# Six sums of an MLP block written for GpSimd instead of VectorE, and four pieces of the block in other places

## The chip, the cores and the metric

The kernel runs on one core of one Trainium2 chip. A core has five engines that run their own instruction streams and meet only at semaphores: TensorE (PE, with its weight loads PEld), VectorE (DVE), ScalarE (ACT), GpSimd (POOL) and SyncE (SP). Sixteen DMA engines move data between the core's memory and HBM. The metric is device time in microseconds (us) of one execution.

## The reference

A decoder trunk of two layers over 256 tokens of width 2048, all in fp32. Layer 0 mixes with a gated linear recurrence, layer 1 with attention; after each mixer comes an MLP with a squared ReLU, and then a gated embedding. The part that the change touches is the MLP:

```python
def sq_relu_mlp(u, w_up, w_down):
    hid = jax.nn.relu(u @ w_up)
    return (hid * hid) @ w_down      # w_up 2048 x 8192, w_down 8192 x 2048
```

## The kernel before

**Precision by splitting.** A weight tile arrives from HBM as fp32. ScalarE rounds it into a tile `whi` (line 113, a CAST), VectorE subtracts to get the remainder `wlo` (line 114), and TensorE makes three products of the parts. The helper `split` records both lines, and there are four buffers of each of `whi` and `wlo`: the cast of a tile waits until TensorE is done with the tile four places ahead of it. A product therefore waits for DMA, ScalarE and VectorE in that order, and the three engines work only a few tiles ahead of TensorE.

**The MLP in blocks.** The hidden width is cut into eight blocks of 1024. For a block, `up` is called eight times: 48 matmuls for 128 hidden columns, then on VectorE the ReLU and the norm's scale (line 304), on ScalarE the square (306), and the split of the squares into `hid` (237, 238). The down projection of a block is not done as eight plain products but in the manner of Strassen and Winograd: a product of two by two parts is made from seven products of half the size, for which sums of parts are formed first.

- Sums of the activations: after every second `up`, lines 317, 318 and 319 form four combinations of `squares` into `scr` (128x256, then twice 128x128), lines 321 (ScalarE) and 322 (VectorE) split them.
- Sums of the weights: many are made by the transfer itself (`accum_op=ALU.add` in `load`, line 283, issued from GpSimd's queue into `chain` and `chq`). Three are made by an engine: line 403 adds the two halves of `chain` (two instructions of 128x1024), line 429 adds a freshly loaded `raw` to `chq`, and line 436 adds a part of `chain` to it (128x1536 each).

The pieces of a block's down projection have names: `p1` to `p7` (two weight tiles of 1024 columns each, 12 matmuls of 512 columns), `r1` to `r7` (tiles of 1024 and 512 columns, 9 matmuls), `m0` and `m1` (one tile, 12 matmuls). Most leave their product in a bank `pp`, from which VectorE adds it into an accumulator (line 338); `r2`, `r3`, `r4`, `m0` and `m1` accumulate in banks `pn` that stay.

**The order.** While block b's `up` products run, block b-1's pieces run between them, in the order of one list of words (line 467). TensorE follows it exactly, since every matmul there is tied behind the one before. For the other engines a scheduler orders the instructions when the kernel is built, by modelled times; at run time each engine takes its own in that order, and an instruction that waits holds up all that stand behind it on the same engine. Two of the sums, 429 and 436, are also tied behind the last `wlo` (`behind`, line 104).

Of the kernel before, what the change touches and what calls it, by code (L numbers as in the profile page):

```python
# [14 lines left out]
ALU = mybir.AluOpType  # L15
# [20 lines left out]
def yoco_kernel(ctx, tc, a, out):  # L36
    nc = tc.nc
# [43 lines left out]
    def slot_flat(which, name, back=0):  # L81

        pool, shift = (late, 28) if which == "C" else (big, 60)
        t = pool.tile([P, KC * 2 * T + 64], F32R, name=name, tag="slot" + which, bufs=1)
        return t[:, shift - back : shift - back + KC * 2 * T]


    def load_slab(src, n, parts, before=None):

        raw = wp.tile([P, D], F32, name="raw", tag="raw", bufs=3)  # L90
        m = n // parts
        if not before:
            nc.sync.dma_start(raw[:, :n], src)
        got = []
        for i in range(parts):
            r = raw[:, i * m : (i + 1) * m]
            if before:
                before[i]()
                nc.sync.dma_start(r, src[:, i * m : (i + 1) * m])
            got.append(split(r, m))  # L100
        return got
# [3 lines left out]
    def behind(ins, name):  # L105

        tc.add_manual_dep(ins.ins, order[name].name, mybir.DependencyInfo(mybir.DependencyClass.NoSync, mybir.DependencyReason.DATA), reason="order")
# [28 lines left out]
    def mm_split(pairs, act, kcs=KC, off=0, ps=None, mm=nc.tensor.matmul):  # L136
        if ps is None:
            ps = psm.tile([P, T], F32, name="ps", tag="mm")
        for k in range(kcs):
            kk = k + off  # L140
            pair, kl = pairs[kk // 8], kk % 8
            st, sp = k == 0, k == kcs - 1
            mm(ps, wk(pair, kl, 0), act[:, k, 0, :], start=st, stop=False)  # L143
            mm(ps, wk(pair, kl, 0), act[:, k, 1, :], start=False, stop=False)  # L144
            mm(ps, wk(pair, kl, 1), act[:, k, 0, :], start=False, stop=sp)  # L145
        return ps
# [103 lines left out]
    def mlp(layer, u, stats, slots, u2, g2, pool, pps):  # L250
# [21 lines left out]
        chq = pool.tile([P, 1536], F32, name="chq", tag="chq", bufs=1)  # L272
        cq = cB[:, :1536]
# [17 lines left out]
        def up(b, i):  # L291

            n = i // 2 + i % 2 * 4
            if n == 0:
                f = slot_flat(slots[b % 2], f"hid{layer}_{b}", 0 if b == NBL - 1 else 24)
                nf = f[:, : 8 * 2 * T].rearrange("p (k w t) -> p k w t", w=2, t=T)
                sf = f[:, 8 * 2 * T :].rearrange("p (j f w t) -> p j f w t", j=4, f=4, w=2)
                hid[b] = nf, sf
            nf, sf = hid[b]
            ps = mm_split(load_slab(a["w_up"][layer, b * 8 + n], D, 2), u, mm=line)  # L300
            if not rs:
                rs.append(stats.rstd())
            t = scr[:, :T]
            nc.vector.scalar_tensor_tensor(t, ps, 0.0, rs[0], op0=ALU.max, op1=ALU.mult)
            s = squares[:, i % 2, :]
            nc.scalar.activation(s, t, AF.Square)
            plain_split(nf, n, s)
            if b == NBL - 1:
                return
            if n < 4:  # L310
                return

            x = scr[:, T:].rearrange("p (f t) -> p f t", f=4)
            a11, a12 = (squares[:, i, :P] for i in range(2))
            a21 = squares[:, 0, P:].unsqueeze(1).broadcast_to([P, 2, P])
            both = squares.rearrange("p i t -> p (i t)").rearrange("p (g t) -> p g t", t=P)[:, 0::3]
            nc.vector.tensor_tensor(x[:, 0:2], a21, both, op=ALU.subtract)
            nc.vector.tensor_tensor(x[:, 2], a11, x[:, 1], op=ALU.subtract)
            nc.vector.tensor_tensor(x[:, 3], a12, x[:, 2], op=ALU.subtract)
            o = sf[:, n - 4]  # L320
            nc.scalar.copy(o[:, :, 0, :], x)
            nc.vector.tensor_tensor(o[:, :, 1, :], x, o[:, :, 0, :].bitcast(F32), op=ALU.subtract)
# [31 lines left out]
        def halves(r):  # L354
            return chunks(r, 4)
# [11 lines left out]
        def down(b):  # L367

            nf, sf = hid[b]

            def plain(half, tok):
                return lambda j: tuple(nf[:, 4 * half + j, w, tok * P : (tok + 1) * P] for w in range(2))

            def form(i):
                return lambda j: tuple(sf[:, j, i, w, :] for w in range(2))

            def one(name, op, pairs):
                o = psm.tile([P, 512], F32, name="pp", tag="mm")
                product(o, op, pairs, True)
                into(name, o)  # L380

            last = b == NBL - 2
            add = dict(accum_op=ALU.add)

            def p1():
                load(nc.gpsimd, cA, quarter(b, 0, 0))
                load(nc.gpsimd, cB, quarter(b, 1, 4))
                pairs = halves(cA)
                load(nc.gpsimd, cA, quarter(b, 0, 4), **add)
                one("1", plain(0, 0), pairs)  # L390

            def p3():
                one("3", form(S4), halves(cB))

            def p2():
                one("2", plain(1, 0), loaded(quarter(b, 1, 0)))

            def p5():
                one("5", form(S1), halves(cA))

                for i in range(2):
                    v, w = (x.rearrange("p (n k c) -> p k n c", n=4, k=4)[:, 2 * i : 2 * i + 2] for x in (cA, cB))
                    nc.vector.tensor_tensor(v, v, w, op=ALU.add)
                load(nc.gpsimd, cB, quarter(b, 0, 4), **add)

            def p7():
                one("7", form(S3), halves(cB))
                load(nc.gpsimd, cq, quarter(b, 1, 12, f=fr))

            def p6():  # L410
                pairs = halves(cA)
                load(nc.gpsimd, cA, quarter(b, 1, 0), **add)
                one("6", form(S2), pairs)

            def p4():
                one("4", plain(1, 1), halves(cA))

            def r1():
                load(nc.gpsimd, chq, quarter(b, 0, 8, f=fr))
                pairs = chunks(chq, 3)  # L420
                load(nc.gpsimd, chq, quarter(b, 0, 12, f=fr), **add)
                one("r1", plain(0, 0), pairs)

            def r2():
                r = raw_tile()[:, :1536]
                load(nc.sync, r, quarter(b, 1, 8, f=fr))
                product(nbank[0][0], plain(1, 0), chunks(r, 3), False, last)

                behind(nc.vector.tensor_tensor(chq, chq, r, op=ALU.add), "lo")  # L429

            def r5():
                one("r5", form(S1), chunks(chq, 3))

            def r3():
                product(nbank[1][0], form(S4), chunks(cq, 3), False, last)
                behind(nc.vector.tensor_tensor(chq, chq, cq, op=ALU.add), "lo")
                load(nc.gpsimd, cq, quarter(b, 0, 12, f=fr), **add)

            def r6():
                one("r6", form(S2), chunks(chq, 3))  # L440

            def r4():
                product(nbank[0][1], plain(1, 1), chunks(chq, 3), False, last)

            def r7():
                one("r7", form(S3), chunks(cq, 3))

            def m(q):

                raw = raw_tile()[:, :1024]  # L450
                load(nc.sync, raw, quarter(b, q, 8, 8, fm))
                hi, lo = split(raw, 1024)
                for c in range(2):
                    cols = slice(c * 512, (c + 1) * 512)
                    for t in range(2):

                        product(nbank[c][t], lambda j: plain(q, t)(3), [(hi[:, cols], lo[:, cols])], b == q == 0, last and q == c == t == 1)

            return dict(p1=p1, p2=p2, p3=p3, p4=p4, p5=p5, p6=p6, p7=p7, r1=r1, r2=r2, r3=r3,
                        r4=r4, r5=r5, r6=r6, r7=r7, m0=lambda: m(0), m1=lambda: m(1))  # L460

        for n in range(8):
            up(0, n)
        for b in range(1, NBL):
            d = down(b - 1)
            n = 0
            for item in "up p1 up p3 r1 up p5 m0 p6 up r5 up p7 p2 p4 m1 up r3 up r6 r2 up r4 r7".split():
                if item == "up":
                    up(b, n)
                    n += 1  # L470
                else:
                    d[item]()
# [614 lines left out]
```

## Time and profile before

| | us |
|---|---|
| median of 3 runs | 2432.49 (2432.47 to 2432.61) |
| the profiled execution | 2432.98 |
| its span, first to last instruction | 2431.2 |
| TensorE busy in the span | 2404.9 |
| VectorE, ScalarE, GpSimd busy | 1937.2, 1474.8, 157.9 |
| granted TensorE clock, mean | 0.997 |

There are seven blocks with both `up` and down work in each of the two MLPs, 14 in all. They repeat with a period of 83.76 us. Below, a place in a block is shown in the block from 863.36 to 947.12 us of the profiled execution. A row of the timeline has the start, the duration, the engine, the line, the operation, and the tiles written and read; a row of groups ends with the busy time and the mean duration in ns, then with the idle time of the engine before such instructions.

### The profile page before, as it was taken

How to read it: one execution, taken by the hardware profiler on the slowest of the kernel's cores; microseconds unless marked ns; L12 is line 12 of the kernel's file. 1: busy time of each engine (PE TensorE's matmuls, PEld its weight loads, DVE VectorE, ACT ScalarE, POOL GpSimd, SP SyncE). 2: the span in 40 equal slices, each digit the busy share in tenths (PEclk: the TensorE clock that was granted, in tenths of full speed). 3: DMA queues.
4: the chain of work that ended last, by engine and by line, in shares of the span. 5: the costliest groups of instructions: out<-in, count | busy, mean ns of one | idle time of the engine just before them, and what ended most of it. 6: DMA issues, size and time to landing. Idle time of an engine off the chain costs nothing.

```text
span 2431.2 us, 43771 instructions
## 1 busy us (share of the span) xinstructions
PE 2404.9 (99%) x17898; PEld 2285.2 (94%) x17898; DVE 1937.2 (80%) x2914; ACT 1474.8 (61%) x2224; POOL 157.9 (6%) x201
## 2 busy tenths in 40 slices
PE   9999999999999999999999999999999999999998
PEld 8999999999999999899999999999999999989998
DVE  7897797678888888889874566667888888888976
ACT  6666575566666666656664555556666666665664
POOL 1000000001110111110000000000011011111000
PEclk9999999999999999999999999999999999999999
DMA  6554545578888887886555655557888888788653
GB/s 243 175 182 174 186 179 208 196 235 250 231 226 243 239 230 234 251 213 230 189 184 183 206 178 179 180 196 246 237 232 235 241 246 219 237 246 225 226 191 122
DMA packets 148985, 518.07 MB, mean 213 GB/s; under 512 B 9136, under 2 KB 59888, under 8 KB 111408
## 3 DMA queue, kind: packets, MB, share of 16 engines
q1 hardware_dynamic: 95200, 382.62, 44.2%
q0 software_dynamic: 52288, 130.62, 23.6%
q8 instruction: 140, 2.29, 0.4%
q10 hardware_dynamic: 1296, 2.03, 0.2%
q14 instruction: 61, 0.50, 0.1%
HBM read 508.91 MB, written 6.32 MB: 212 GB/s over the span
## 4 chain that ended last, share of the span: by engine, by line
PE 96%; DVE 2%; issue 1%; ACT 0%; DMA 0%; POOL 0%; DVEq 0%; POOLq 0%
PE ps L131 29%; PE pp L131 15%; PE ps L143 12%; PE ps L145 12%; PE ps L144 12%; PE pst L131 7%; PE pn L131 6%; DVE wlo L114 1%; DVE chq L429 0%; ACT whi L113 0%; PE pu L143 0%; PE pu L144 0%; PE pu L145 0%; DVE accr L338 0%; PE pa L741 0%
## 5 line engine op out<-in xcount | busy, mean ns | idle before, releaser
L113 ACT CAST whi<-raw 128x1024 fp32r<-128x1024 f32 (+2 forms) x742 | 763.3, 1033 | 667.9 <-PE ps L144 280.1
L114 DVE TENSOR_TENSOR wlo<-raw,whi 128x1024 fp32r<-128x1024 f32 (+2 forms) x742 | 886.6, 1200 | 329.2 <-ACT whi L113 323.5
L131 PE MATMUL ps<-u_m,whi 128*128 128x256 f32 x4096 | 707.3, 276 | 0.0
L131 PEld LDWEIGHTS ps<-u_m,whi 128*128 128x128 f32 x4096 | 626.0, 188 | 8.7
L131 PE MATMUL ps<-u_m,wlo 128*128 128x256 f32 x2048 | 566.4, 277 | 9.0 <-DVE wlo L114 8.8
L131 PEld LDWEIGHTS ps<-u_m,wlo 128*128 128x128 f32 x2048 | 384.6, 188 | 11.8 <-DVE wlo L114 11.8
L131 PE MATMUL pp<-whi,hid 128*128 128x512 f32 x1120 | 364.1, 390 | 0.0
L113 ACT CAST whi<-chain 128x1024 fp32r<-128x1024 f32 x224 | 221.1, 997 | 137.6 <-PE ps L131 89.2
L114 DVE TENSOR_TENSOR wlo<-chain,whi 128x1024 fp32r<-128x1024 f32 x224 | 256.7, 1156 | 28.4 <-ACT whi L113 26.8
L131 PEld LDWEIGHTS pp<-whi,hid 128*128 128x128 f32 x1120 | 210.2, 188 | 41.3
L131 PE MATMUL pp<-wlo,hid 128*128 128x512 f32 x560 | 218.5, 390 | 0.0
L143 PE MATMUL ps<-u_a,whi 128*128 128x256 f32 x768 | 213.6, 278 | 0.0
L145 PE MATMUL ps<-u_a,wlo 128*128 128x256 f32 x768 | 211.9, 276 | 0.0
L144 PE MATMUL ps<-u_a,whi 128*128 128x256 f32 x768 | 211.9, 276 | 0.0
L131 PE MATMUL pn<-whi,hid 128*128 128x512 f32 x476 | 158.2, 390 | 0.0
L283 POOL DMA_DIRECT2D chain<-in_w_down x98 | 104.0, 1061 | 749.7 <-DVE wlo L114 302.3
L143 PEld LDWEIGHTS ps<-u_a,whi 128*128 128x128 f32 x768 | 144.3, 188 | 0.2
L144 PEld LDWEIGHTS ps<-u_a,whi 128*128 128x128 f32 x768 | 144.3, 188 | 0.2
L145 PEld LDWEIGHTS ps<-u_a,wlo 128*128 128x128 f32 x768 | 144.2, 188 | 0.1
L143 PE MATMUL ps<-u_p,whi 128*128 128x256 f32 x512 | 141.2, 276 | 0.0
L145 PE MATMUL ps<-u_p,wlo 128*128 128x256 f32 x512 | 140.9, 275 | 0.0
L144 PE MATMUL ps<-u_p,whi 128*128 128x256 f32 x512 | 140.9, 275 | 0.0
(294 smaller groups left out, 4712.7 us busy)
## 6 DMA issues: line engine op xcount, KB each, us to landing
raw<-in_w_up SPq DMA_DIRECT2D x128, 1024.0 KB, 5.6
chain<-in_w_down POOLq DMA_DIRECT2D x70, 1024.0 KB, 9.4
raw<-in_w_ain SPq DMA_DIRECT2D x48, 1024.0 KB, 4.8
raw<-in_w_pg SPq DMA_DIRECT2D x32, 1024.0 KB, 4.8
raw<-in_w_down SPq DMA_DIRECT2D x30, 1024.0 KB, 5.4
chq<-in_w_down POOLq DMA_DIRECT2D x28, 768.0 KB, 6.5
chain<-in_w_down POOLq DMA_DIRECT2D x28, 768.0 KB, 6.5
raw<-in_w_vf SPq DMA_DIRECT2D x20, 832.0 KB, 4.4
```

Of the source, the lines that this page charges most:

```text
L113: nc.scalar.copy(h_, r)
L114: order["lo"] = nc.vector.tensor_tensor(l_, r, h_.bitcast(F32), op=ALU.subtract).ins
L131: ins = nc.tensor.matmul(*args, **kw).ins
L143: mm(ps, wk(pair, kl, 0), act[:, k, 0, :], start=st, stop=False)
L144: mm(ps, wk(pair, kl, 0), act[:, k, 1, :], start=False, stop=False)
L145: mm(ps, wk(pair, kl, 1), act[:, k, 0, :], start=False, stop=sp)
L283: eng.dma_start(dst.rearrange("p (n f) -> p n f", f=src.shape[-1]), src, **kw)
```

## The change

Lines 317, 318, 319, 403, 429 and 436 are issued on GpSimd instead of VectorE. The ties of 429 and 436 to the last `wlo` go with it. In the list of words, `p6` goes behind the next `up`, `m1` ahead of `p4`, and `r7` ahead of `r4`.

```diff
-            nc.vector.tensor_tensor(x[:, 0:2], a21, both, op=ALU.subtract)
-            nc.vector.tensor_tensor(x[:, 2], a11, x[:, 1], op=ALU.subtract)
-            nc.vector.tensor_tensor(x[:, 3], a12, x[:, 2], op=ALU.subtract)
+            nc.gpsimd.tensor_tensor(x[:, 0:2], a21, both, op=ALU.subtract)
+            nc.gpsimd.tensor_tensor(x[:, 2], a11, x[:, 1], op=ALU.subtract)
+            nc.gpsimd.tensor_tensor(x[:, 3], a12, x[:, 2], op=ALU.subtract)
...
-                    nc.vector.tensor_tensor(v, v, w, op=ALU.add)
+                    nc.gpsimd.tensor_tensor(v, v, w, op=ALU.add)
...
-                behind(nc.vector.tensor_tensor(chq, chq, r, op=ALU.add), "lo")
+                nc.gpsimd.tensor_tensor(chq, chq, r, op=ALU.add)
...
-                behind(nc.vector.tensor_tensor(chq, chq, cq, op=ALU.add), "lo")
+                nc.gpsimd.tensor_tensor(chq, chq, cq, op=ALU.add)
...
-            for item in "up p1 up p3 r1 up p5 m0 p6 up r5 up p7 p2 p4 m1 up r3 up r6 r2 up r4 r7".split():
+            for item in "up p1 up p3 r1 up p5 m0 up p6 r5 up p7 p2 m1 p4 up r3 up r6 r2 up r7 r4".split():
```

The built programs show how the instructions stand. The first place is VectorE at the end of a block, before the change: the splits of `r6` (`chq`), of `r2` (the `raw` tiles of 1024 and 512 columns), the sum 429, and then the splits of the last `up` (the `raw` pair) and of `r4` and `r7`.

```order
L114 TENSOR_TENSOR wlo<-chq,whi 128x512
L319 TENSOR_TENSOR scr<-sqrs,scr 128x128
L114 TENSOR_TENSOR wlo<-raw,whi 128x1024
L322 TENSOR_TENSOR hid_4_9287<-scr,hid_4_9287 128x4x128
L304 SCALAR_TENSOR_TENSOR scr<-ps,rstd 128x256
L114 TENSOR_TENSOR wlo<-raw,whi 128x512
L429 TENSOR_TENSOR chq<-chq,raw 128x1536
L238 TENSOR_TENSOR hid_4_9287<-sqrs,hid_4_9287 128x256
L338 TENSOR_TENSOR accr_7442<-accr_7442,pp 128x512
L114 TENSOR_TENSOR wlo<-raw,whi 128x1024 x2
```

With the change the same stretch of VectorE, and what follows up to the first `up` of the next block (the second `raw` pair):

```order
L114 TENSOR_TENSOR wlo<-chq,whi 128x512
L322 TENSOR_TENSOR hid_4_9287<-scr,hid_4_9287 128x4x128
L114 TENSOR_TENSOR wlo<-raw,whi 128x1024
L304 SCALAR_TENSOR_TENSOR scr<-ps,rstd 128x256
L114 TENSOR_TENSOR wlo<-raw,whi 128x512
L238 TENSOR_TENSOR hid_4_9287<-sqrs,hid_4_9287 128x256
L338 TENSOR_TENSOR accr_7442<-accr_7442,pp 128x512
L114 TENSOR_TENSOR wlo<-raw,whi 128x1024 x2
L114 TENSOR_TENSOR wlo<-chain,whi 128x1024
L114 TENSOR_TENSOR wlo<-chain,whi 128x512
L114 TENSOR_TENSOR wlo<-chq,whi 128x1024
L304 SCALAR_TENSOR_TENSOR scr<-ps,rstd 128x256
```

The sums 319 and 429 are gone from it, 322 stands one split earlier, and `r7`'s splits (`chain`) stand ahead of `r4`'s (`chq`).

The third place is GpSimd's queue. Before, it holds transfers alone; with the change a block reads as follows, from the sums of the sixth `up` on:

```order
L317 TENSOR_TENSOR scr<-sqrs 128x256
L318 TENSOR_TENSOR scr<-sqrs,scr 128x128
L319 TENSOR_TENSOR scr<-sqrs,scr 128x128
L429 TENSOR_TENSOR chq<-chq,raw 128x1536
L283 DMA chain<-in_w_down 128x4x512
L317 TENSOR_TENSOR scr<-sqrs 128x256
L283 DMA chq<-in_w_down 128x4x384
L318 TENSOR_TENSOR scr<-sqrs,scr 128x128
L319 TENSOR_TENSOR scr<-sqrs,scr 128x128
L283 DMA chain<-in_w_down 128x4x512
L317 TENSOR_TENSOR scr<-sqrs 128x256
L283 DMA chq<-in_w_down 128x4x384
```

Every transfer of the down weights that GpSimd issues now stands behind sums that wait for ScalarE or for other transfers.

## The prediction

> **What bounds the kernel now.** I read the page first, then the waits of TensorE and of its weight loads, then the timeline of one block. The page:
>
> ```profile
> PE 2404.9 (99%) x17898; PEld 2285.2 (94%) x17898; DVE 1937.2 (80%) x2914; ACT 1474.8 (61%) x2224; POOL 157.9 (6%) x201
> ```
>
> TensorE is busy for 2404.9 us of a span of 2431.2 us, and the change leaves its products as they are. All that any order of the other engines can win is what TensorE waits for. The list of waits, of TensorE and of its weight loads (us in total, times, longest):
>
> ```profile
> PE ps L131 <- DVE wlo L114: 8.8, 12, 0.7
> PEld ps L131 <- DVE wlo L114: 11.8, 14, 0.9
> ```
>
> Inside the MLPs there is one wait that repeats: an `up` product waits for its remainder `wlo` from VectorE, 12 times. The timeline of one of them, where `r6` (into `pp`) ends, `r2` (into `pn`) follows, and then the block's last `up` (into `ps`) begins:
>
> ```profile
> 929.31 0.68 DVE L114 TENSOR_TENSOR wlo<-chq,whi 128x512 fp32r<-128x512 f32 x1
> ...
> 932.04 0.69 DVE L322 TENSOR_TENSOR hid<-scr,hid 128x512 fp32r<-128x512 f32 x1
> ...
> 932.64 0.42 DVE L304 SCALAR_TENSOR_TENSOR scr<-ps,rstd 128x256 f32<-128x256 f32 x1
> ...
> 933.18 0.69 DVE L114 TENSOR_TENSOR wlo<-raw,whi 128x512 fp32r<-128x512 f32 x1
> ...
> 933.79 1.75 DVE L429 TENSOR_TENSOR chq<-chq,raw 128x1536 f32<-128x1536 f32 x1
> ...
> 934.02 2.01 ACT L113 CAST whi<-raw 128x1024 fp32r<-128x1024 f32 x2
> ...
> 934.28 0.39 PE L131 MATMUL pp<-whi,hid 128*128 128x512 f32 x1
> ...
> 935.46 0.42 DVE L238 TENSOR_TENSOR hid<-sqrs,hid 128x256 fp32r<-128x256 f32 x1
> ...
> 935.80 0.68 DVE L338 TENSOR_TENSOR accr<-accr,pp 128x512 f32<-128x512 f32 x1
> ...
> 936.06 1.57 ACT L113 CAST whi<-chq 128x1024 fp32r<-128x1024 f32 x2
> ...
> 936.39 2.35 DVE L114 TENSOR_TENSOR wlo<-raw,whi 128x1024 fp32r<-128x1024 f32 x2
> ...
> 936.54 0.39 PE L131 MATMUL ps<-u_m,whi 128*128 128x256 f32 x2
> 937.66 0.19 PEld L131 LDWEIGHTS ps<-u_m,wlo 128*128 128x128 f32 x1 [0.93 <-DVE wlo L114]
> 937.66 0.38 PE L131 MATMUL ps<-u_m,wlo 128*128 128x256 f32 x1 [0.73 <-DVE wlo L114]
> ...
> 943.04 0.40 PE L131 MATMUL pn<-whi,hid 128*128 128x512 f32 x1
> ```
>
> The sum 429 takes VectorE from 933.79 to 935.54. Behind it stand 238, 338 and then the remainder that TensorE needs; that one ends at about 937.6, and TensorE goes on at 937.66. The product took from 936.54 to 943.04, 6.50 us, and an undisturbed one takes 5.48 us (the second of the next two fences). So each stall is worth 1.0 us, and twelve are 12.0 us, 0.5% of the time. That is the ceiling of the gain. How full the engines are in the block, and the undisturbed `up`:
>
> ```profile
> 863.36:947.12 83.76, 83.03 (x556) 76.02 (x555) 73.74 (x94) 52.15 (x68) 9.48 (x9) 1.00 0.82 236
> ```
> ```profile
> 919.59 5.48 PE ps L131 x48
> ```
>
> (Window, length, then busy time of PE, PEld, DVE, ACT, POOL.) VectorE has 10 us of 83.76 free, GpSimd 74.
>
> **The change part by part: what leaves VectorE.**
>
> ```profile
> L317 DVE TENSOR_TENSOR scr<-sqrs 128x256 f32<-128x256 f32 x56 | 23.4, 418 | 0.0
> L318 DVE TENSOR_TENSOR scr<-sqrs,scr 128x128 f32<-128x128 f32 x56 | 16.0, 286 | 0.0
> L319 DVE TENSOR_TENSOR scr<-sqrs,scr 128x128 f32<-128x128 f32 x56 | 16.3, 291 | 1.1
> L403 DVE TENSOR_TENSOR chain<-chain 128x1024 f32<-128x1024 f32 x28 | 34.1, 1219 | 0.0
> L429 DVE TENSOR_TENSOR chq<-chq,raw 128x1536 f32<-128x1536 f32 x14 | 24.5, 1752 | 0.0
> L436 DVE TENSOR_TENSOR chq<-chq,chain 128x1536 f32<-128x1536 f32 x14 | 24.5, 1753 | 0.0
> ```
>
> Together 138.8 us, 9.9 us a block. Only 429 lies on the path that sets the end; the others are hidden behind TensorE, and taking them away is worth nothing by itself. With 429 gone, 238 goes as soon as its cast is done, and 338 waits for `r6`: its last product starts at 934.28 and lasts 0.39, so 934.67. Then 0.59 for 338 (as from 935.80 to 936.39) and 1.2 for the split: the remainder ends at 936.5. TensorE asks for it 0.12 after 936.54 (between two matmuls of that kind lie 5.48/48 = 0.11 us). So the stall of 1.0 us goes, but only 0.1 us is left as reserve: 338, which waits for TensorE itself, is late next.
>
> The new order puts `r7` (which needs 338) ahead of `r4` (which does not), so the first `up` of the next block stands exactly so: a 9-matmul product that is added by 338, another 9 matmuls, the `up`. The reserve there is also about 0.1 us.
>
> **What the sums cost on GpSimd.** The trace has no such operation there. The nearest rows are its selections with one input, and its work beside VectorE's. In order: two selections with VectorE idle (by mean over 8, and one), then two beside it, and two of VectorE's lines undisturbed:
>
> ```profile
> L589 POOL TENSOR_SCALAR_AFFINE_SELECT mD<-mD 32x32 f32<-32x32 f32 x8 | 1.6, 205 | 0.3
> ```
> ```profile
> 3.09 0.32 POOL masks.py:199 TENSOR_SCALAR_AFFINE_SELECT ident<-ident 128x128 f32<-128x128 f32 x1
> ```
> ```profile
> 1264.87 0.56 POOL L883 TENSOR_SCALAR_AFFINE_SELECT cmask<-cmask 128x128 f32<-128x128 f32 x1
> 1265.19 0.51 DVE L234 SCALAR_TENSOR_TENSOR u_q<-h,gains,u_q 128x256 fp32r<-128x256 f32 x1
> 1265.39 0.47 POOL L886 TENSOR_SCALAR_AFFINE_SELECT tri<-tri 128x128 f32<-128x128 f32 x1
> 1265.63 0.51 DVE L187 TENSOR_TENSOR ssq<-ssq,sq 128x256 f32<-128x256 f32 x1
> ```
> ```profile
> 1244.13 0.48 DVE L234 SCALAR_TENSOR_TENSOR u_q<-h,gains,u_q 128x256 fp32r<-128x256 f32 x1
> ...
> 1244.53 0.41 DVE L187 TENSOR_TENSOR ssq<-ssq,sq 128x256 f32<-128x256 f32 x1
> ```
>
> From 32 to 128 elements: (0.32-0.205)/96 = 1.2 ns each and 0.17 us fixed. My estimate takes two inputs as twice that: 3.8 us for 1536 elements, 2.6 for 1024, 0.8 for 256, 0.5 for 128. The lower bound is VectorE's own 1.75 us for 1536; the upper is the estimate times 0.56/0.32, 6.7 us. A block's sums are then 4 x 1.8 + 2 x 2.6 + 2 x 3.8 = 20 us, and with the 9.48 us of transfers GpSimd is busy for 30 of 83 us. The Trainium skill, GPSIMD Engine Reference, section 3.1, gives 4497 ns for an addition of 2048 elements; in proportion 1536 would be 3.4 us, and the sum of this prediction would be the same by it.
>
> **What GpSimd takes from VectorE.** Beside a selection of 128 elements one instruction of VectorE took 0.03 us more (0.51 against 0.48) and another 0.10 more (0.51 against 0.41). I read it as 0.03 to 0.10 us lost for each 128 elements that GpSimd reads, mid 0.065. Two places have no reserve:
>
> - The last `up`. Sum 429 reads 2 x 1536 elements, 24 times 128: 0.7 to 2.4 us, mid 1.6, if VectorE is busy throughout. It starts when `r6`'s last split is over (929.99) and by the estimate is done by 933.8, ahead of the split that TensorE waits for. From 929.99 to 934.67 VectorE has 0.69+1.2+0.42+0.69+0.42 = 3.4 us of work, so 1.2 us are free, and about seven tenths of the time is busy: a loss of 1.1 mid, 1.7 at the upper end. Against 1.2 that is a stall of 0 mid, 0.5 at most.
> - The first `up`. Only 318 and 319 fall on its split, 512 elements read: 4 x 0.065 = 0.26 mid, 0.4 at most, less 0.07 of reserve: 0.2 us mid, 0.33 at most.
>
> Elsewhere I cost the contention at nothing, since 403 and 436 leave 2.4 and 1.75 us on VectorE at the very places where GpSimd now makes them.
>
> **New waits.** On ScalarE, 321 waits for 319 on GpSimd, and the casts of the next piece (`p1`, `p5`, `p7`, `r2`) queue behind it. The casts of `p6` wait for 403, those of `r4` for 429. Both pieces were moved back, `p6` by an `up` (5.48 us) against 2 x (2.6-1.2) = 2.8 us more for 403; `r4` was cast at 936.06 and now comes 2 us later, while 429 ends at 933.8. GpSimd's queue is in order, so the accumulating transfer behind 403 goes out up to 2.8 us later. Its reserve:
>
> ```profile
> 889.87 1.26 POOL L283 DMA_DIRECT2D chain<-in_w_down  x1 [9.79 <-DVE chain L403]
> ```
> ```profile
> 902.61 1.05 ACT L113 CAST whi<-chain 128x1024 fp32r<-128x1024 f32 x1 [0.17 <-ACT sqrs L306]
> ```
> ```profile
> 908.52 0.40 PE L131 MATMUL pp<-whi,hid 128*128 128x512 f32 x1
> ```
> ```profile
> chain<-in_w_down POOLq DMA_DIRECT2D x70, 1024.0 KB, 9.4
> ```
>
> Issued at 889.87 and landing 9.4 later it is there at 899.3, cast at 902.61 for a product at 908.52. With 2.8 us more it lands at 902.1, still ahead of the cast, behind which 3.6 us more are free (908.52-902.61 less 1.05 and 1.2). These edits come at no cost; at the upper durations (2 x 4.6 us for 403) the transfer would be 6.8 us late, which 3.3 + 3.6 still cover.
>
> **The sum.** 12 stalls x 1.0 = -12.0; first `up`, 14 x 0.2 = +2.8; the rest 0. The profiled execution's 2432.98 becomes 2423.8. The median lies 0.49 below that execution, so I forecast **2423.3 us**, 0.4% faster; own range 2420.4 (no new stall) to 2427.6.
>
> **The rivals.**
>
> - **Nothing measurable** (the waits only change hands). At the upper end of the contention, 0.5 us at the last `up` and 0.33 at the first are left: 14 x 0.83 = 11.6 against 12.0 won, 2432 us. For it: two reserves of 0.1 us. Against: it takes the worse of two rows at both places.
> - **Slower, by exclusion.** VectorE's remainder has two inputs in the core's memory. If it may not run while GpSimd reads there at all, the 3.8 us of 429 hold up `r2`'s and the last `up`'s splits: 3.8 less 1.2 free less 0.1 is 2.5 us in the place of 1.0, +1.5 x 12 = 18 us, 2450.5 us. It decides from 2.2 us of hold on (1.2+1.0). For it: the selections too took 0.56 and 0.47 against 0.32. Against: VectorE lost at most 0.10 us to either, a fifth of the selection. The Trainium skill has this rule: SBUF — State Buffer, section Who interferes with whom, says that a VectorE instruction with two SBUF inputs contends with a GpSimd instruction that reads SBUF and that one blocks the other fully; the trace agrees that both lose, but not that VectorE waits for all of it.
> - **Slower, by GpSimd's queue.** If 403 takes over 4.6 us, the transfer behind it comes after the cast's reserve, and `p7` waits: at 5 us each, 2 x 3.8 = 7.6 us later against 6.9 of reserve, 0.7 us a block, 10 us, ending near 2433. Little speaks for it.
>
> **How the numbers follow.** Forecast 0.60, nothing measurable 0.20, exclusion 0.16, queue 0.04. About 0.2% (4.9 us) can be told from no change. Faster than 2427.6: 0.60 and a little of the second case, 0.62. Within: most of the second, part of the fourth, 0.19. Slower: exclusion and part of the others, 0.19. The range takes the forecast's own, the second case and the mild end of exclusion: 2420.3 to 2440.
>
> **What would show it.** Right: no wait of `ps` for `wlo` at the last `up`; period 82.8 to 83.0 us instead of 83.76; splits near 1.22 us except beside GpSimd; 429 between 3 and 5 us on GpSimd. Wrong: splits of 2 us and more beside 429 and a wait as long as before (exclusion); 338 released by TensorE with the split behind it late (second case); `whi` waiting for a landing of `chain` (queue).

## The result and the profile after

The changed kernel takes 2475.66 us (median of 5 runs, 2475.12 to 2476.59), the kernel before in the same runs 2432.47 us (2431.91 to 2432.61). The ratio is 1.0178 with an interval of 1.0163 to 1.0193: 43.2 us slower, where 9.2 us faster was forecast. The time is above the whole predicted range.

The page of the changed kernel, first its span, then the busy times:

```profile
span 2473.9 us, 43978 instructions
...
PE 2424.4 (98%) x17898; PEld 2285.2 (92%) x17898; DVE 1997.5 (81%) x2690; ACT 1474.8 (60%) x2224; POOL 511.9 (21%) x425
```

The telling number is VectorE's. It had 1937.2 us of work, six sums worth 138.8 us were taken from it, and it is now busy for 1997.5 us, not 1798.4. Its other instructions have grown by 199 us. ScalarE's busy time is what it was to the tenth (1474.8).

TensorE's waits (us in total, times, longest) show where that ends:

```profile
PE pn L131 <- DVE wlo L114: 11.9, 14, 1.1
PE ps L131 <- DVE wlo L114: 10.9, 15, 0.8
PE pp L131 <- DVE wlo L114: 7.6, 13, 0.8
```

The one wait of before, 12 times at `up` (`ps`), is still there, 15 times now, and two have joined it: `pn` is `r2`, behind sum 429, and `pp` is `p4`, behind sum 436. These three rows are 30.4 us against 8.8, about half of what was lost. Much of the rest stands in TensorE's busy time, which went from 2404.9 to 2424.4 us: a matmul that had to wait is shown longer too (0.50 us in the place of 0.39 in the row for `r2` below). The waits of the weight loads hold more of it:

```profile
PEld pn L131 <- DVE wlo L114: 17.9, 14, 1.5
PEld ps L131 <- DVE wlo L114: 16.5, 24, 1.0
PEld pp L131 <- DVE wlo L114: 13.1, 13, 1.3
PEld ps L131 <- ACT whi L113: 6.9, 14, 0.5
```

Together they are 54.4 us, where the one row of before had 11.8: 42.6 us more, beside a loss of 43.2. The measure is rough: with the weights' sums alone, below, such rows grow by 39.5 us for a loss of 34.8. One period of a block, from one last `up` to the next, has grown from 83.76 to 87.00 us at the same granted clock (1.00; the columns are those of the prediction's window):

```profile
866.24:953.24 87.00, 84.60 (x555) 76.03 (x555) 78.30 (x78) 52.12 (x67) 35.42 (x25) 1.00 0.81 227
```

The groups say which instructions grew. The first four rows are GpSimd's sums, the others VectorE's:

```profile
L403 POOL TENSOR_TENSOR chain<-chain 128x1024 f32<-128x1024 f32 x28 | 91.7, 3290 | 51.8 <-DVE wlo L114 51.8
L317 POOL TENSOR_TENSOR scr<-sqrs 128x256 f32<-128x256 f32 x56 | 59.9, 1069 | 218.2 <-ACT sqrs L306 218.1
L436 POOL TENSOR_TENSOR chq<-chq,chain 128x1536 f32<-128x1536 f32 x14 | 56.3, 4025 | 73.8 <-DMA chain<-in_w_down 73.8
L429 POOL TENSOR_TENSOR chq<-chq,raw 128x1536 f32<-128x1536 f32 x14 | 49.4, 3530 | 18.0 <-DVE wlo L114 18.0
...
L114 DVE TENSOR_TENSOR wlo<-chain,whi 128x1024 fp32r<-128x1024 f32 x196 | 279.5, 1447 | 8.9 <-ACT whi L113 8.9
L322 DVE TENSOR_TENSOR hid<-scr,hid 128x512 fp32r<-128x512 f32 x56 | 78.2, 1397 | 4.0 <-ACT hid L321 2.4
L238 DVE TENSOR_TENSOR hid<-sqrs,hid 128x256 fp32r<-128x256 f32 x128 | 77.0, 602 | 9.3 <-ACT hid L237 4.5
L338 DVE TENSOR_TENSOR acc<-acc,pp 128x512 f32<-128x512 f32 x84 | 57.0, 678 | 0.0
```

Lines 322 and 238 took 0.69 and 0.42 us before, in the mean they now take 1.40 and 0.60. Line 338, which adds a product out of TensorE's banks, takes the 0.68 us it always did. Few of its instructions run beside a sum, though. Line 304 does in every block; it too has one input in a bank:

```profile
898.07 6.68 POOL L403 TENSOR_TENSOR chain<-chain 128x1024 f32<-128x1024 f32 x2 [3.50 <-DVE wlo L114]
902.40 0.41 DVE L304 SCALAR_TENSOR_TENSOR scr<-ps,rstd 128x256 f32<-128x256 f32 x1
```

It takes 0.41 us in the middle of a sum, while the splits just ahead of it and behind it take 3.43 and 3.10 us in the place of 1.22. So VectorE isn't slowed as such: lines with both inputs in the core's memory are, and a line with one input in a bank is not.

The minima, medians and maxima of two lines, each from the view of a single line (ns; VectorE's remainders first, GpSimd's sum 429 behind):

```profile
L114 DVE TENSOR_TENSOR wlo<-chain,whi x224: 677/1216/4560, 527.6 to 2308.4; 128x1024 fp32r<-128x1024 f32 x112
```
```profile
L429 POOL TENSOR_TENSOR chq<-chq,raw x14: 3517/3532/3532, 596.9 to 2296.4; 128x1536 f32<-128x1536 f32 x14
```

The median split is unchanged (1.22 us), the longest takes 4.56. It is not that all are a little slower: a few are late by a whole sum.

The timeline at the two places, VectorE first and then GpSimd. The upper rows are the splits of `p4` with sum 436, the lower ones the end of the block with 429:

```profile
926.30 5.68 DVE L114 TENSOR_TENSOR wlo<-chain,whi 128x1024 fp32r<-128x1024 f32 x2
931.91 0.68 DVE L338 TENSOR_TENSOR acc<-acc,pp 128x512 f32<-128x512 f32 x1
...
943.74 0.95 DVE L114 TENSOR_TENSOR wlo<-chq,whi 128x512 fp32r<-128x512 f32 x1
944.83 4.02 DVE L322 TENSOR_TENSOR hid<-scr,hid 128x512 fp32r<-128x512 f32 x1
948.77 1.21 DVE L114 TENSOR_TENSOR wlo<-raw,whi 128x1024 fp32r<-128x1024 f32 x1
```
```profile
926.37 4.53 POOL L436 TENSOR_TENSOR chq<-chq,chain 128x1536 f32<-128x1536 f32 x1 [4.91 <-DMA chain<-in_w_down]
943.61 0.53 POOL L319 TENSOR_TENSOR scr<-sqrs,scr 128x128 f32<-128x128 f32 x1
944.76 3.53 POOL L429 TENSOR_TENSOR chq<-chq,raw 128x1536 f32<-128x1536 f32 x1 [0.63 <-DVE wlo L114]
```

429 runs from 944.76 to 948.29. Line 322 begins 0.07 us behind it and ends at 948.85, 0.56 us after the sum is over; alone it takes 0.69. It did practically nothing while the sum ran. The same distance comes back wherever a sum was under way first: the 28 splits of 1024 columns that meet 403 so end 1.08 to 1.09 us after it, and the 44 instructions of line 238 that meet 317 end 0.28 us after it. With 436 it is VectorE that begins first, by 0.07 us: GpSimd's sum then takes 4.53 us, 1.0 more than 3.53, which is the rest of the first split, and the second split takes the remaining 4.5 of the pair's 5.68 us. TensorE's rows for `r2`, which needs the split at 948.77, and for the last `up` behind it:

```profile
950.04 0.50 PE L131 MATMUL pn<-wlo,hid 128*128 128x512 f32 x1 [0.92 <-DVE wlo L114]
...
953.47 0.39 PE L131 MATMUL ps<-u_m,wlo 128*128 128x256 f32 x1 [0.76 <-DVE wlo L114]
```

That is the picture of the rival "slower, by exclusion". It could still be something else: GpSimd's longer queue, the writes, the new places, or the squares' sums. The experiments separate these.

### The profile page after: what moved, and what is told of

It is laid out like the page before. It is cut to its first block, busy times and chain, and to the rows that moved or that the text cites. A ratio compares the mean times of both kernels' runs of the same rounds, so it can differ in the third digit from the quotient of the medians.

```text
span 2473.9 us, 43978 instructions
## 1 busy us (share of the span) xinstructions
PE 2424.4 (98%) x17898; PEld 2285.2 (92%) x17898; DVE 1997.5 (81%) x2690; ACT 1474.8 (60%) x2224; POOL 511.9 (21%) x425
## 4 chain that ended last, share of the span: by engine, by line
PE 86%; DVE 6%; issue 4%; ACT 2%; POOL 1%; DMA 0%; DVEq 0%; ACTq 0%; POOLq 0%
PE ps L131 26%; PE ps L145 12%; PE ps L143 12%; PE ps L144 12%; PE pp L131 11%; PE pst L131 7%; DVE wlo L114 4%; PE pn L131 3%; ACT whi L113 1%; POOL scr L317 1%; POOL scr L318 1%; DVE acc L338 0%; ACT sqrs L306 0%; DVE accr L338 0%; PE pu L143 0%
## 5 line engine op out<-in xcount | busy, mean ns | idle before, releaser
L114 DVE TENSOR_TENSOR wlo<-raw,whi 128x1024 fp32r<-128x1024 f32 (+2 forms) x742 | 953.8, 1291 | 299.9 <-ACT whi L113 294.9
L131 PE MATMUL ps<-u_m,wlo 128*128 128x256 f32 x2048 | 570.0, 278 | 11.7 <-DVE wlo L114 10.9
L114 DVE TENSOR_TENSOR wlo<-chain,whi 128x1024 fp32r<-128x1024 f32 x224 | 297.4, 1351 | 8.9 <-ACT whi L113 8.9
L113 ACT CAST whi<-chq 128x1024 fp32r<-128x1024 f32 x112 | 93.8, 838 | 138.6 <-PE ps L131 111.6
L143 PE MATMUL ps<-u_p,whi 128*128 128x256 f32 x512 | 141.2, 276 | 0.0
```

The lines of the kernel that those rows point to most:

```text
L113: nc.scalar.copy(h_, r)
L114: order["lo"] = nc.vector.tensor_tensor(l_, r, h_.bitcast(F32), op=ALU.subtract).ins
L131: ins = nc.tensor.matmul(*args, **kw).ins
```

## The experiments

Theory: **exclusion**, a VectorE instruction with two inputs in the core's memory and a GpSimd instruction that reads there do not run together, and the later one waits for the whole of the earlier one. Rivals: a loss in proportion (both go on, each slower), the queue, and the order. All times are medians with the ratio to the kernel before of the same runs (2432.47 to 2432.55 us).

### The order alone, and the sums alone

The order of the change with the sums on VectorE, that is the kernel before with

```diff
-            for item in "up p1 up p3 r1 up p5 m0 p6 up r5 up p7 p2 p4 m1 up r3 up r6 r2 up r4 r7".split():
+            for item in "up p1 up p3 r1 up p5 m0 up p6 r5 up p7 p2 m1 p4 up r3 up r6 r2 up r7 r4".split():
```

> All sums stay on VectorE, the four pieces stand in the new places. Exclusion (a VectorE instruction with two SBUF inputs waits for a whole GpSimd instruction that reads SBUF): the order is not the cause; sum 429 still holds up the last up, 12 stalls of 1.0 us stay, 2430 to 2435 us. Order (the new places cost by themselves, as 338 now stands ahead of the first split of the next block): most of the loss is here, 2455 to 2476 us.

2434.13 us, ratio 1.0006 (0.9996 to 1.0015). The wait at the last `up` is as before:

```profile
PE ps L131 <- DVE wlo L114: 8.8, 12, 0.7
```

And the reverse, the change with the old list of words:

> All six sums on GpSimd, the pieces in the old places. Exclusion: as slow as the whole change or slower, since p6 then follows sum 403 at once and r4 sum 429, 2470 to 2495 us. Order: 2425 to 2435 us.

2505.47 us, 1.0299 (1.0281 to 1.0316), above the range I expected. The new places are worth nothing where VectorE makes the sums and save 30 us where GpSimd makes them; the whole cost is the sums'.

### The two kinds of sums apart

On the new order, only lines 317 to 319 on GpSimd:

```diff
-            nc.vector.tensor_tensor(x[:, 0:2], a21, both, op=ALU.subtract)
-            nc.vector.tensor_tensor(x[:, 2], a11, x[:, 1], op=ALU.subtract)
-            nc.vector.tensor_tensor(x[:, 3], a12, x[:, 2], op=ALU.subtract)
+            nc.gpsimd.tensor_tensor(x[:, 0:2], a21, both, op=ALU.subtract)
+            nc.gpsimd.tensor_tensor(x[:, 2], a11, x[:, 1], op=ALU.subtract)
+            nc.gpsimd.tensor_tensor(x[:, 3], a12, x[:, 2], op=ALU.subtract)
```

> New places; the sums of squares 317 to 319 on GpSimd, the sums of weights on VectorE. Exclusion: holds of 0.9 and twice 0.5 us, four times a block, against 4.0 us taken off VectorE; where VectorE has reserve they cost nothing, so the stall of 1.0 us behind 429 stays and little comes to it: 2430 to 2442 us. By the run with the sums of weights alone (2467.4) the rest of the whole change's loss, 8 us, would come from here: 2440.

2434.1 us, 1.0008 (0.9999 to 1.0018): nothing. Busy times with the order alone, and with these sums moved:

```profile
PE 2406.6 (99%) x17898; PEld 2286.3 (94%) x17898; DVE 1937.8 (80%) x2914; ACT 1477.7 (61%) x2224; POOL 157.9 (6%) x201
```
```profile
PE 2406.8 (99%) x17898; PEld 2286.1 (94%) x17898; DVE 1931.5 (79%) x2746; ACT 1480.8 (61%) x2224; POOL 312.9 (13%) x369
```

VectorE gave up 55.7 us of sums (23.4 + 16.0 + 16.3) and got back 49 of it in longer instructions; TensorE did not notice.

The weights' sums alone (the change with 317 to 319 back on VectorE):

> New places; the sums of weights 403, 429 and 436 on GpSimd, the sums of squares 317 to 319 on VectorE. Exclusion: the long holds (3.5 us for 1536 elements, 2.4 for 1024) make the loss, so most of the 43 us stays: 2460 to 2480 us. If the many short sums are the cause: 2430 to 2445 us.

2467.36 us, 1.0145 (1.013 to 1.016): 34.8 of the 43.2 us.

### GpSimd as long at work, but without reading

As the last kernel, but each sum of weights is replaced by fills of the same tile, two for each half of 403 and three for 429 and for 436. The sums of weights are left out, so their reads are too; the queue, the writes and the waits that the writes bring stay:

```diff
-                    nc.gpsimd.tensor_tensor(v, v, w, op=ALU.add)
+                    for _ in range(2):
+                        nc.gpsimd.memset(v, 0.5)
...
-                nc.gpsimd.tensor_tensor(chq, chq, r, op=ALU.add)
+                for _ in range(3):
+                    nc.gpsimd.memset(chq, 0.5)
...
-                nc.gpsimd.tensor_tensor(chq, chq, cq, op=ALU.add)
+                for _ in range(3):
+                    nc.gpsimd.memset(chq, 0.5)
```

> As the run with the sums of weights alone on GpSimd, but each sum replaced by fills of its target on GpSimd (two for 403, three for 429 and 436, about as long or longer than the sums): the sums of weights and their reads are left out, the products are made with the fills. Exclusion: GpSimd reads nothing, VectorE is not held, the stall behind 429 is gone too: 2419 to 2426 us, and all splits of 1024 near 1.22 us. Queue (GpSimd too slow, its transfers and the casts behind it late): GpSimd is busy as long, so 2455 to 2480 us.

2422.08 us, 0.9957 (0.9942 to 0.9972). Two of the groups of fills, and VectorE's splits in the view of the single line (those with `raw` as input; those of `chain` and `chq` take at most 1.226 and 1.227 us):

```profile
L431 POOL MEMSET chq<- 128x1536 f32 x42 | 58.2, 1385 | 96.3 <-DVE wlo L114 94.7
L404 POOL MEMSET chain<- 128x1024 f32 x56 | 52.7, 955 | 68.9 <-DVE wlo L114 67.3
```
```profile
L114 DVE TENSOR_TENSOR wlo<-raw,whi x742: 678/1224/1228, 9.6 to 2395.8; 128x1024 fp32r<-128x1024 f32 x175, 128x832 fp32r<-128x832 f32 x10, 128x512 fp32r<-128x512 f32 x1
```

GpSimd is at work for 4.2 us (3 x 1.385) where the sum took 3.5, and none of these splits takes longer than 1.228 us. The fills do run beside such lines: line 322 begins during a fill of 431 in 12 blocks and takes 0.68 us there. So it is not the queue, and not GpSimd's being busy or writing. What is left is that the sums read; a fill and a sum also differ in the operation, and no experiment has GpSimd read in another way (the two selections of the prediction, read again below, are the only such rows). The time itself, 10.5 us under before, comes near the ceiling that the prediction set at 12.0.

### The same reads in small pieces

As the weights alone, each sum in instructions of 256 elements (429 shown; 436 and 403 likewise):

```diff
-                nc.gpsimd.tensor_tensor(chq, chq, r, op=ALU.add)
+                for k in range(0, 1536, 256):
+                    nc.gpsimd.tensor_tensor(chq[:, k : k + 256], chq[:, k : k + 256], r[:, k : k + 256], op=ALU.add)
```

> As the sums of weights alone on GpSimd, but each in pieces of 256 elements (six for 429 and 436, four for a half of 403). If the hold lasts one GpSimd instruction: no split of 1024 takes longer than 1.22 + 0.9 = 2.1 us, but all pieces together hold longer (6 x 0.87 = 5.2 us against 3.5) and VectorE is held once per instruction: the time stays between 2440 and 2475 us, the longest splits fall from 4.5 to about 2.1 us. If the hold lasted as long as GpSimd has work queued: splits of 4.5 us and more as before, 2467 us or more.

2437.79 us, 1.0021 (1.0012 to 1.003), just under the range that I expected. Splits and the pieces of 429:

```profile
L114 DVE TENSOR_TENSOR wlo<-raw,whi x742: 687/1225/1823, 9.9 to 2412.4; 128x1024 fp32r<-128x1024 f32 x175, 128x832 fp32r<-128x832 f32 x10, 128x512 fp32r<-128x512 f32 x1
```
```profile
L432 POOL TENSOR_TENSOR chq<-chq,raw 128x256 f32<-128x256 f32 x84 | 91.0, 1109 | 49.6 <-DVE wlo L114 49.6
```

GpSimd reads as much as before and is at it for longer (6 x 1.11 = 6.7 us against 3.5), yet the loss falls from 34.8 to 5.3 us, and the longest split takes 1.82 us (1.77 with `chain` as input), where the weights' sums in one piece each have 4.38 (4.57 with `chain`). A loss in proportion to what is read would have stayed. What counts is the length of one instruction: a split waits for one piece and then has its turn. Still nothing is won: TensorE waits for the last `up`'s remainder 12 times, 12.1 us in all.

### Each sum of weights by itself

On the new order, with one line on GpSimd at a time (429 here, then 436, then 403):

```diff
-                behind(nc.vector.tensor_tensor(chq, chq, r, op=ALU.add), "lo")
+                nc.gpsimd.tensor_tensor(chq, chq, r, op=ALU.add)
```

> New places, only sum 429 on GpSimd. Exclusion, from the run with the sums of weights alone (r2 1.0 us longer there, the last up 1.1, its stall of before 1.0): about 1.1 us a block more than before, 14 blocks: 2442 to 2452 us. If the loss came from all sums in sum and not from the place: a third of 35 us, also about 2444; told apart by where TensorE waits: at r2 and the last up alone.

> New places, only sum 436 on GpSimd; 429 stays on VectorE with its stall of 1.0 us. Exclusion: p4 waits 0.7 to 0.9 us and the up behind it 0.3, 14 blocks: 2444 to 2452 us, with splits of 4.5 us beside 436 alone.

> New places, only sum 403 (two instructions of 1024) on GpSimd; 429 stays on VectorE with its stall. Exclusion: splits of 3.3 us beside 403, but TensorE's reserve there is 2 to 3 us and two sums of 1.2 us leave VectorE: 2433 to 2437 us, the least harm of the three.

| on GpSimd | time, us | against before, us | ratio (interval) |
|---|---|---|---|
| 429 alone | 2449.55 | +17.0 | 1.0070 (1.0055 to 1.0085) |
| 436 alone | 2447.86 | +15.3 | 1.0066 (1.0049 to 1.0082) |
| 403 alone | 2434.89 | +2.3 | 1.0009 (1.0000 to 1.0019) |
| the three (as above) | 2467.36 | +34.8 | 1.0145 (1.013 to 1.016) |

They add up: 17.0 + 15.3 + 2.3 = 34.6. All four have the new order; measured against the order alone (2434.13) they are 15.4, 13.7 and 0.8, in sum 29.9 of 33.2, so the sum holds to within some 3 us. The waits of TensorE with 429 alone, and the split that it holds in the timeline of all engines:

```profile
PE ps L131 <- DVE wlo L114: 10.6, 14, 0.8
PE ps L131 <- ACT whi L113: 6.1, 12, 0.5
```
```profile
935.57 3.55 POOL L429 TENSOR_TENSOR chq<-chq,raw 128x1536 f32<-128x1536 f32 x1 [4.80 <-DVE wlo L114]
936.38 3.82 DVE L114 TENSOR_TENSOR wlo<-raw,whi 128x1024 fp32r<-128x1024 f32 x1 [0.70 <-ACT whi L113]
```

The sum ends at 939.12, `r2`'s first split at 940.20, 1.08 later, nearly its whole 1.22. With 436 alone, TensorE's waits and VectorE's timeline:

```profile
PE ps L131 <- DVE wlo L114: 8.8, 12, 0.7
PE pp L131 <- DVE wlo L114: 6.6, 13, 0.8
```
```profile
916.57 0.42 DVE L238 TENSOR_TENSOR hid<-sqrs,hid 128x256 fp32r<-128x256 f32 x1
916.91 5.68 DVE L114 TENSOR_TENSOR wlo<-chain,whi 128x1024 fp32r<-128x1024 f32 x2
922.51 0.67 DVE L338 TENSOR_TENSOR acc<-acc,pp 128x512 f32<-128x512 f32 x1
923.11 2.35 DVE L114 TENSOR_TENSOR wlo<-raw,whi 128x1024 fp32r<-128x1024 f32 x2
```

The first row is 429's old wait, untouched; the second is new. VectorE has no gap from 916.57 to 925.5 there, so what the sum takes from it goes straight on to `p4` and the `up` behind it. With 403 alone no wait comes up that repeats: its holds are covered.

### Two ways to have the gain

Is the sum at 429 better made by VectorE after the last `up`'s splits? The new order, all sums on VectorE, and 429 tied behind these splits:

```diff
-                behind(nc.vector.tensor_tensor(chq, chq, r, op=ALU.add), "lo")
+                late_sum.append((chq, r))
...
             def r7():
+                q_, r_ = late_sum.pop()
+                behind(nc.vector.tensor_tensor(q_, q_, r_, op=ALU.add), "lo")
                 one("r7", form(S3), chunks(cq, 3))
```

> All sums on VectorE, new places, and sum 429 recorded with r7 behind the splits of the last up instead of with r2 ahead of them. If the only thing to win was the 1.75 us of 429 ahead of the split that TensorE waits for: the stall goes without GpSimd, 2420 to 2425 us. If the wait only goes on to the first up of the next block (338 and the sums of squares now stand ahead of its split): 2426 to 2434 us.

2421.6 us, 0.9954 (0.9942 to 0.9967), faster than both kernels, 10.9 us under before. All of TensorE's waits of 1 us and more; each comes once:

```profile
PE ps_ssqc L206 <- DVE sq L181: 2.0, 1, 2.0
PE pst L131 <- DVE wlo L114: 1.9, 1, 1.9
PE pst L131 <- ACT whi L113: 1.8, 1, 1.8
PE warm L64 <- POOL ones L60: 1.1, 1, 1.1
PE ps_spread L215 <- DVE diag L214: 1.0, 1, 1.0
```

Or by a transfer inside the core's memory, which adds `raw` to `chq`; GpSimd only issues it (its busy time grows by 12.7 us, 0.9 for each):

```diff
-                behind(nc.vector.tensor_tensor(chq, chq, r, op=ALU.add), "lo")
+                nc.gpsimd.dma_start(chq, r, **add)
```

> All sums on VectorE except 429, which is made by a transfer that adds raw to chq inside the core's memory (issued from GpSimd, 1.3 us). Exclusion is about instructions that read through the shared interface, and a transfer does not hold VectorE: stall gone, 2420 to 2425 us, if the transfer lands within about 9 us (r4's cast is 9 us behind r6's last split). If it is slower, the cast of r4 waits: 2430 us and more.

2422.47 us, 0.9958 (0.9946 to 0.9971); no wait repeats either. The transfers (KB each, median us from issue to landing):

```profile
chq<-raw POOLq DMA_DIRECT2D x14, 768.0 KB, 8.3
```

## Why the prediction was wrong, step by step

**The ceiling (12.0 us): right.** Three kernels without the wait at the last `up` end 10.5, 10.9 and 10.1 us under before. The step that read 12 waits of 1.0 us as the only thing to win stands; the 12.0 is 10 to 20% too much.

**What leaves VectorE: right in substance.** 429 is the one sum on the path, and 403, 436 and 317 to 319 were hidden; moving 429 alone on VectorE gives the whole gain.

**The sums' cost on GpSimd: right.** I estimated 3.8 us for 1536 elements and the undisturbed sum takes 3.53; the shortest 317 takes 0.86 against 0.8, 319 at 128 elements 0.53 against 0.5. The view of the single line 317 in the change:

```profile
L317 POOL TENSOR_TENSOR scr<-sqrs x56: 860/874/1471, 498.6 to 2224.8; 128x256 f32<-128x256 f32 x56
```

The estimate in proportion from the Trainium skill (GPSIMD Engine Reference, section 3.1) was 3.4 us; 3.53 is nearer to it than my own 3.8.

**What GpSimd takes from VectorE: this step failed, twice.** First the kind. I took 0.03 to 0.10 us for each 128 elements from instructions of VectorE beside a short selection, and scaled it by what is read. For 429 this gave "a loss of 1.1 mid, 1.7 at the upper end", against 1.2 us that were free. The runs show that a split loses what is left of the sum at its start, up to all 3.5 us: 4.02 us in the place of 0.69, and most of the loss goes with short instructions though the reads are the same. The row that I held against exclusion did not speak against it. Line 187 was recorded from 1265.63, while line 234 ahead of it still ran until 1265.70, and the selection was over at 1265.86. Only some 0.16 us of the selection could hold it up at all, and it lost 0.10. I set that against the whole 0.47 and called it "a fifth"; it was most of what could be seen. Where the two rows end says more than how long they took: line 234 ends 0.27 us after the selection ahead of it (1265.70 and 1265.43), line 187 0.28 us after the other (1266.14 and 1265.86). Both are of 128x256 with two inputs in the core's memory, as line 238 is, and line 238 ends 0.28 us after the sum that holds it. So the old rows already fit exclusion. They are two, and no run repeated the selections.

Second, the place. The sentence "Elsewhere I cost the contention at nothing, since 403 and 436 leave 2.4 and 1.75 us on VectorE at the very places" set off what leaves VectorE against a loss by the wrong rate. By 3.5 us of hold, 436 costs 1.8 net at a place where VectorE runs without a gap: 15.3 us by itself, almost as much as 429. For 403 the same argument held (2 x 2.4 us of hold against 2.4 freed, and +2.3 us measured), because that place has reserve, not because the contention is small.

**The first `up` (+2.8 us): not seen where it was predicted.** With the squares' sums alone nothing is lost there. But they are not free beside the weights' sums: the whole change takes 8.3 us more than the weights' sums alone. In the change, 429 starts just ahead of line 322 in 12 blocks and holds it, so that `r2`'s split, which stands behind, comes late; with the weights' sums alone, 322 takes at most 0.69 us and `pn` waits twice for 0.9 us in all, against 14 times for 11.9. With the weights' sums alone, the row of TensorE's waits and that of the single line 322:

```profile
PE pn L131 <- DVE wlo L114: 0.9, 2, 0.4
```
```profile
L322 DVE TENSOR_TENSOR hid<-scr,hid x56: 676/683/687, 501.6 to 2221.9; 128x512 fp32r<-128x512 f32 x56
```

The listed waits of TensorE on the MLPs grow by only about 5 of the 8.3 us between these two kernels (7.6 + 10.9 + 11.9 against 10.6 + 7.8 + 6.1 + 0.9), and TensorE's busy time grows by 1.0 (2423.4 to 2424.4). What makes the rest stays open.

**New waits, the queue and the order: right to cost them at nothing.** The fills keep GpSimd's queue as long and lose nothing; the order alone is 1.0006.

**The rivals.** "Slower, by exclusion" is what happens. Its condition ("decides from 2.2 us of hold on") was met with 3.5, and its price for 429, 2450.5 us, is close to what 429 alone measures, 2449.55. That it is so close is partly luck: I wrote 12 stalls of 1.5 us more, and the 17.0 us are 1.2 more in each of 14 blocks. It was priced at one place. With the measured 15.3 us of 436, 2.3 of 403 and 8.3 of the squares beside them in addition it would have been 2476. I gave it 0.16. Its rule in the Trainium skill (SBUF — State Buffer, section Who interferes with whom) was the one I set aside with "the trace agrees that both lose, but not that VectorE waits for all of it"; it says that one blocks the other fully. The trace of the change agrees with that: 944.76 to 948.29 for the sum, 948.85 for the end of 322. By the same section of the Trainium skill a VectorE instruction with at most one input there does not contend, outside its 2-port performance modes, which no run here shows apart; the trace agrees, as line 304 keeps its 0.41 us beside 403.

The two observations that I named against myself, splits of 2 us and more beside 429 and a wait that stays, are the ones that came.

## What to carry to other kernels

Moving elementwise work from VectorE to an idle GpSimd was no gain here, where VectorE's other instructions read two operands from the core's memory. VectorE loses what is left of each GpSimd sum that is under way when one of them begins. So estimate the price as GpSimd's duration, less what leaves VectorE there and less the reserve, at every place and not only at the one that was meant. Look first whether the same work fits VectorE later, or a transfer (10.9 and 10.1 us won here). If it must be moved, cut it into short instructions (a loss of 5.3 us instead of 34.8). And to judge a contention from a short row, set the loss against the overlap of the two rows, not against the length of either, and see whether the one always ends at the same distance behind the other.

## What the hardware showed that I had not expected

- The hold goes both ways and by who starts first: beside a split that began 0.07 us earlier, sum 436 took 4.53 us against 3.53.
- Fills by GpSimd hold nothing: 4.2 us of them beside the same splits leave the splits at 1.23 us or less.
- A transfer that adds 768 KB within the core's memory lands after 8.3 us and costs the kernel nothing that its time shows (2422.47 against 2421.6 us with the late sum on VectorE).
